# A two-layer attention and state-space trunk on one core: all hi and lo halves of q and k and all Toeplitz blocks moved to DMA transfers, a second token block sharing one PSUM bank, and a new instruction order

## The chip, the cores and the metric

The kernel runs on 1 core of a Trainium2 chip. The metric is the device time of one execution in microseconds (us), and lower is better. Before the change the median of three executions is 1128.52 us (1127.23 to 1130.73).

## The reference

The model is two post-norm layers on x of 512 tokens by 1024 features, float32. Cut to what matters:

```python
for l in range(2):
    h = x @ w_in[l]                                   # 1024 -> 2048
    q, k, v, u = jnp.split(h, [512, 1024, 1536], axis=-1)
    # attention: 4 heads, each with two maps of width 64; rotary on q and k; causal
    a = softmax(q0 @ k0.T / 8) - lam * softmax(q1 @ k1.T / 8)
    attn_out = rms_norm(a @ v, subln_g[l]) * (1 - lam_init)
    # S5: 32 groups of 16 channels, a complex diagonal state of 64 each, then GELU and GLU
    states = associative_scan(a_bar, einsum(u, b_bar))
    y = gelu(real(einsum(states, c)) + d_skip * u)
    ssm_out = y * sigmoid(y @ glu_w[l] + glu_b[l])
    mix = concat([attn_out, ssm_out]) @ w_out[l]
    x = layer_norm(ALPHA * x + mix, ln1_g[l], ln1_b[l])
    ff = square(relu(x @ w_ff1[l])) @ w_ff2[l]        # 1024 -> 4096 -> 1024
    x = layer_norm(ALPHA * x + ff, ln2_g[l], ln2_b[l])
```

## The kernel before

**Arithmetic.** Large products run as three fp32r matmuls, a.hi b.hi + a.hi b.lo + a.lo b.hi (`mm3`). A weight tile of 128x1024 is loaded into a `raw` buffer, rounded by ScalarE to `whi`, and its remainder becomes `wlo` in one of three ways, chosen by a letter: V (VectorE subtracts), P (GpSimd subtracts), A (ScalarE writes -hi and a GpSimd-issued accumulating DMA adds raw). The letters of the projections stand in `PLAN["lo"]`, of w_ff1 in `flo` (by i mod 4), of w_ff2 in `glo` (by the product m of a Strassen-like scheme of seven products) and `elo`, of w_out in `nlo`.

**Stages of a layer.** The projection list `back` names units: q and k of head h (`qkproj`, lines 1022 to 1068), v (`vproj`), u (`uproj`), and the GLU (`glu`). Between them come the attention units (`attn_u`, line 1110: head h, token block b of 128 queries), and the S5 units (`ssm_pars`, `ssm_outp`, `ssm_a`, `ssm_b`, `ssm_c`). Then come w_out with the first LayerNorm, and the feed-forward part in 8 chunks, each of four `ffone` (w_ff1) and seven `fftwo` (w_ff2) units, the last one `ffend` with the second LayerNorm.

**q and k.** After the projection ScalarE copies the PSUM bank to `src`, four DMAs swap 32-row blocks into `swp`, and VectorE makes the rotary result in three operations. The split into hi and lo halves for the two maps has two forms, chosen by `PLAN["qm"][l]`, first letter q and second k. In form A ScalarE casts 64-row pieces into the `xq` tiles (two for q, four for k), VectorE makes two 64-row remainders, and for k GpSimd clears two halves. In form D ScalarE casts all 128 rows once, VectorE makes one 128-row remainder, and DMAs from the SP queue put the 64-row pieces into their places: four for q, eight for k. Before, layer 0 has D for q and A for k, and layer 1 has A for both.

**Toeplitz blocks.** `ssm_outp` (line 976) fills `mx` with shifted copies of a 128-row block m3. In form A of `PLAN["mm"]` these are six ScalarE copies of 32 rows per call; in form D three DMAs.

**Banks of the attention.** Each map's scores get a PSUM bank of 512 columns. For blocks b below `PLAN["one"]` both maps share one bank: then one mask matmul and one VectorE maximum serve both.

**Order.** All instructions are recorded as `Op` objects with predecessors (`Rec.add`), then a list scheduler (`Rec.run`) simulates five queues with the durations of `Rec.cost` (DMA: lines 291 to 300, contention between the two DMA queues: lines 482 to 488) and issues in the order of the simulated starts. Each queue is in order on the chip. Priorities are shifted by hand-set tables: `pri` by unit, `fine` by instruction, `ao`, `so`, `ap`, `sp`, `po` by kind of unit, and the places of the units in the list by `att` and `s5`. `PE.matmul` fillers on the tile `wz` are added where the simulation leaves TensorE idle (`fill`).

Of the kernel before, what the change touches and what calls it, by code (L numbers as in the profile page):

```python
# [46 lines left out]
    "att": [[8, 11, 15, 19], [8, 12, 15, 18]],  # L47
    "s5": [[1, 13], [10, 14]],
    "bufs": {"slot": 13, "mh": 2, "y": 3, "xq": 13, "at": 4, "rt": 5, "u": 4},
    "ps": {"acc": 2, "sc": 4, "s5": 2},  # L50
    "lo": ["AAAVAAPAAAAVAAAAAAAA", "AAAAAAAAAAAAAPAVAAVP"],
    "eng": {"rope": ["VVV", "VVV"], "tab": ["VVVVVV", "VVVVVV"], "cg": ["VVVV", "VVVV"], "ch": ["VVVV", "VVVV"], "sa": ["PV", "VP"], "sb": ["VVVVVV", "VVVVVV"]},
    "flo": "VPVV",
    "nlo": "APVAVPVA",
    "glo": "APVVAAV",
    "seq": "f m1 m7 f m2 m4 f m6 f m5 m3",
    "elo": "VVVV",
    "wb": 4,
    "s5o": "p1 p0 o0 a0 b0 a1 c0 p2 o1 a2 b1 b2 c1 p3 o2 a3 b3 c2 o3 c3",
    "swq": "S",  # L60
    "ao": [-6000, -8000],
    "so": [2000, 17000],
    "ap": [56500, 92750],
    "sp": [27000, 25000],
# [9 lines left out]
    "po": 10000,  # L74
    "m3": 4,
    "pri": {"1a30": [150500, -9500], "1q1": [18500, 116500], "1v1": [-17500, 5000], "0ssm_a0": [2500, 74000], "0ssm_a1": [43000, -11000], "0ssm_a2": [57000, 85500], "0ssm_a3": [22500, 64500], "0ssm_b0": [2500, -20000], "0ssm_b1": [-4000, 37500], "0ssm_b2": [-500, 43500], "0ssm_b3": [14000, -60500], "0ssm_c0": [40000, 62000], "0ssm_c1": [53500, -21500], "0ssm_c2": [1500, 53500], "0ssm_c3": [58000, 90000], "0ssm_outp0": [-10500, 69500], "0ssm_outp1": [11000, 46500], "0ssm_outp2": [12000, -8000], "0ssm_outp3": [0, 55500], "0ssm_pars0": [-8000, 64000], "0ssm_pars1": [-6000, 13500], "0ssm_pars2": [10500, 43500], "0ssm_pars3": [1000, 30000], "1a10": [64000, 53500], "0a10": [89500, -22000], "0a22": [54500, 10000], "0q1": [-5000, 7500], "0q2": [19500, -19500], "0q3": [-14000, -14000], "0g1": [-28000, 41000], "1ssm_outp3": [-16000, -86000], "0u2": [37500, 17000], "0u3": [98500, 23500], "1a02": [144000, -41500], "1a31": [110000, 103000], "1a21": [80000, 8500], "1a03": [188000, 64500], "1a11": [94500, 72500], "1a13": [76000, -18500], "1a20": [135500, -91500], "1a22": [73500, 7500], "1a23": [185000, -24500], "1a32": [71500, 28000], "1a33": [105000, 129500], "1q3": [-39500, 10000], "0k0": [22500, -9500], "0k2": [-11500, -22000], "0k3": [5500, 25500], "1ssm_load2": [-29500, 49000], "1ssm_a0": [-11000, 39000], "0g3": [-69000, 40500], "0u0": [19000, -33500], "0u1": [64000, -10500], "1u0": [30000, -43500], "1u2": [11000, -7500], "1e3": [17000, 15500], "1a01": [147000, 78000], "0q0": [-1500, 5000], "0v0": [-5500, 55500], "0v1": [87500, 5000], "1e0": [-88000, -24500], "0v2": [55000, 47500], "0a12": [57500, 7000], "0a01": [91000, -21500], "0e1": [14500, 13500], "1ssm_b3": [30500, -18500], "1e1": [17500, 42500], "1g3": [-78500, 97000], "1g1": [22000, 119000], "1ssm_b2": [-75500, 68000], "0a13": [29000, 3500], "1a00": [103000, 29500], "1a12": [81500, 10500], "1v3": [72500, -37500], "1e2": [-44500, -13500], "1k2": [44500, 125500], "1ssm_outp1": [7000, -60500], "1ssm_a1": [22500, 0], "1ssm_a2": [3500, -24500], "1ssm_a3": [-13500, -24000], "1ssm_b0": [46000, 56500], "1ssm_b1": [-76000, -78000], "1ssm_c0": [0, -8500], "1ssm_c1": [26000, 19000], "1ssm_c2": [-21500, 21500], "1ssm_c3": [3500, -9000], "1ssm_load1": [8000, 13000], "1ssm_load3": [-2500, -13500], "1ssm_outp2": [-39500, 42500], "0k1": [-11000, -7500], "0v3": [118000, 30000], "0a31": [-38500, -27000], "0a03": [-10500, 4500], "0a30": [-4000, 47000], "1g0": [-56500, -27000], "1q0": [18000, -49500], "1q2": [87000, 38000], "0a02": [-2500, 30500], "1v2": [13500, -39000], "0e0": [-11000, 28500], "0e3": [27500, 50500], "0g0": [-81500, 59500], "1k0": [-1500, 9000], "1k1": [-11500, -27500], "0g2": [18000, 20000], "0a11": [10500, 36000], "1v0": [17000, 27000], "0e2": [-11500, 75500], "0a33": [76500, 11000], "1g2": [-32000, 19000], "1u3": [-29500, -5500], "0a32": [56000, 49000], "0a00": [44000, -48500], "1k3": [-3500, 35500], "0a20": [91500, 70000], "0a21": [9000, 66500], "0a23": [18000, 53500], "1u1": [-500, -9000]},
# [7 lines left out]
    "qm": ["DA", "AA"],  # L84
    "mm": ["A", "A"],
    "cc": ["AA", "AA", "AA", "AA"],
    "one": 1,
# [100 lines left out]
class Rec:  # L188
# [97 lines left out]
    def cost(self, op, views):  # L286
# [1435 lines left out]
```

## Time and profile before

| | us |
|---|---|
| median of 3 executions | 1128.52 |
| profiled execution, its own time | 1130.64 |
| its span, first to last instruction | 1128.9 |
| TensorE busy in the span | 1101.6 |
| VectorE busy | 919.5 |
| ScalarE busy | 609.3 |
| GpSimd busy | 199.0 |

The page gives busy time of each engine; the stretches are read from the table of windows, what an engine waited for from the lines of the timeline that carry a bracket, and the chain of waits goes back from the end of a stretch to what released each step. PE is TensorE, DVE VectorE, ACT ScalarE, POOL GpSimd, SP the queue that issues most DMAs. Nearly all instructions carry one line number (L534, where a record is replayed), so tiles are told apart by name: `ps_acc`, `ps_sc` and `ps_s` are PSUM banks, `xq` the halves of q and k, `rt` the rotary buffers, `mx` the Toeplitz blocks, `nm` the maxima.

### The profile page before, as it was taken

To read this page: it belongs to the slowest core of one execution; us is meant where nothing else is said; L and a number is where in the kernel's file an instruction comes from. 1 tells how busy PE (TensorE), PEld (TensorE's weight loads), DVE (VectorE), ACT (ScalarE), POOL (GpSimd) and SP (SyncE) were. 2 spreads that over 40 slices of the span, in tenths; PEclk is the share of its full clock that TensorE was granted. 3 is DMA by queue.
4 is the path that set the end of the run, shared out by engine and by line. 5 is a ranking of instruction groups with operands and counts; after the bars stand their busy time and mean duration, and the time that the engine had idled before them with its cause. 6 is when DMAs were issued, how large, how long until landed. Compare 5 with 4: busy or idle time off the path is not lost.

```text
span 1128.9 us, 15944 instructions
## 1 busy us (share of the span) xinstructions
PE 1101.6 (98%) x5738; PEld 929.7 (82%) x5738; DVE 919.5 (81%) x1575; ACT 609.3 (54%) x1060; POOL 199.0 (18%) x180
## 2 busy tenths in 40 slices
PE   9999989999999999999998999999999999999996
PEld 6889867898888888888788878888988888888885
DVE  7999998888778877877973789857778779778877
ACT  6557878246454464455343767952455445454440
POOL 1112111121211211211021221113112103103101
PEclk9999989999999999999999999999999999999999
DMA  9755645334555455465788764652444554565341
GB/s 312 193 138 109 161 124 155 116 112 115 147 159 131 122 164 134 119 178 148 224 226 208 179 163 106 194 145 81 141 131 131 149 149 119 144 159 148 105 130 74
DMA packets 59582, 167.73 MB, mean 149 GB/s; under 512 B 7408, under 2 KB 11888, under 8 KB 59504
## 3 DMA queue, kind: packets, MB, share of 16 engines
q1 hardware_dynamic: 48848, 127.92, 35.6%
q0 software_dynamic: 10656, 38.80, 18.6%
q8 instruction: 45, 0.74, 0.3%
q14 instruction: 33, 0.27, 0.1%
HBM read 112.17 MB, written 9.44 MB: 108 GB/s over the span
## 4 chain that ended last, share of the span: by engine, by line
PE 85%; DVE 6%; DMA 6%; ACT 3%; issue 1%; SPq 0%; POOL 0%; DVEq 0%; POOLq 0%; ACTq 0%
PE ps_acc L534 45%; PE ps_sc L534 28%; PE ps_s L534 12%; DVE slot L534 2%; DMA wlo<-raw 2%; DVE xq L534 1%; DMA rt<-rt 1%; DVE rt L534 1%; DMA raw<-in_w_v_dram 1%; DMA raw<-in_w_u_dram 1%; DMA keep<-xq 1%; DMA xq<-rt 1%; ACT at L534 0%; DMA slot<-in_xt_dram 0%; ACT whi L534 0%
## 5 line engine op out<-in xcount | busy, mean ns | idle before, releaser
L534 ACT CAST whi<-raw 128x1024 fp32r<-128x1024 f32 x222 | 233.3, 1051 | 284.2 <-PE ps_acc L534 177.9
L534 PE MATMUL ps_acc<-xTh,wlo 128*128 128x512 f32 (+1 forms) x712 | 268.5, 378 | 3.0 <-DMA wlo<-raw 1.9
L534 PE MATMUL ps_acc<-xTh,whi 128*128 128x512 f32 (+1 forms) x712 | 269.9, 380 | 0.7 <-ACT xTh L534 0.6
L534 PE MATMUL ps_acc<-xTl,whi 128*128 128x512 f32 (+1 forms) x712 | 268.7, 379 | 0.5 <-DVE xTl L534 0.5
L534 PE MATMUL ps_sc<-whi,slot 128*128 128x512 f32 x784 | 251.4, 390 | 1.3 <-DVE xq L534 1.3
L534 DVE TENSOR_TENSOR wlo<-raw,whi 128x1024 fp32r<-128x1024 f32 x114 | 139.0, 1226 | 56.6 <-ACT whi L534 56.6
L534 PEld LDWEIGHTS ps_sc<-whi,slot 128*128 128x128 f32 x784 | 147.1, 188 | 32.6 <-DVE xq L534 1.3
L534 POOL DMA_DIRECT2D wlo<-raw x74 | 65.0, 879 | 523.1 <-ACT rt L534 168.6
L534 PEld LDWEIGHTS ps_acc<-xTh,wlo 128*128 128x128 f32 x712 | 134.1, 188 | 26.7 <-DMA wlo<-raw 3.4
L534 PEld LDWEIGHTS ps_acc<-xTh,whi 128*128 128x128 f32 x712 | 134.0, 188 | 25.4 <-ACT xTh L534 1.8
L534 PEld LDWEIGHTS ps_acc<-xTl,whi 128*128 128x128 f32 x712 | 134.2, 188 | 24.2 <-DVE xTl L534 1.9
L534 PE MATMUL ps_sc<-wlo,slot 128*128 128x512 f32 x392 | 152.7, 390 | 0.0
L534 DVE TENSOR_TENSOR slot<-slot 128x512 fp32r<-128x512 f32 (+4 forms) x143 | 105.9, 755 | 7.8 <-ACT slot L534 7.0
L534 POOL TENSOR_TENSOR wlo<-raw,whi 128x1024 fp32r<-128x1024 f32 x34 | 85.0, 2501 | 151.5 <-ACT whi L534 124.2
L534 DVE TENSOR_TENSOR xq<-xq,ps_sc 128x512 f32<-128x512 f32 x124 | 83.6, 681 | 25.8 <-PE ps_sc L534 25.8
L534 ACT ACTIVATE wlo<-raw 128x1024 fp32r<-128x1024 f32 x74 | 78.3, 1060 | 29.0 <-PE ps_acc L534 18.5
L534 PEld LDWEIGHTS ps_sc<-wlo,slot 128*128 128x128 f32 x392 | 73.6, 188 | 15.2
L534 DVE TENSOR_TENSOR raw<-raw 128x1024 f32<-128x1024 f32 x56 | 68.2, 1218 | 14.2 <-DMA raw<-in_w_ff_dram 13.5
L534 ACT CAST slot<-slot 128x512 fp32r<-128x512 f32 x56 | 34.6, 618 | 50.9 <-DVE slot L534 48.4
L534 PE MATMUL ps_acc<-wlo,xTh 128*128 128x256 f32 (+1 forms) x176 | 55.6, 322 | 3.1 <-DMA wlo<-raw 3.1
L534 PE MATMUL ps_acc<-whi,xTh 128*128 128x256 f32 (+1 forms) x176 | 56.3, 324 | 0.2 <-ACT rt L534 0.2
L534 PE MATMUL ps_acc<-whi,xTl 128*128 128x256 f32 (+1 forms) x176 | 55.9, 321 | 0.0
(228 smaller groups left out, 1846.1 us busy)
## 6 DMA issues: line engine op xcount, KB each, us to landing
raw<-in_w_ff_dram SPq DMA_DIRECT2D x128, 512.0 KB, 3.6
wlo<-raw POOLq DMA_DIRECT2D x74, 512.0 KB, 5.3
raw<-in_w_qk_dram SPq DMA_DIRECT2D x16, 512.0 KB, 5.0
raw<-in_w_out_dram SPq DMA_DIRECT2D x16, 512.0 KB, 3.6
raw<-in_w_u_dram SPq DMA_DIRECT2D x8, 512.0 KB, 4.8
raw<-in_w_v_dram SPq DMA_DIRECT2D x8, 512.0 KB, 7.0
rt<-rt SPq DMA_DIRECT2D x64, 64.0 KB, 2.8
at<-in_ln_dram SPq DMA_DIRECT2D x16, 256.0 KB, 3.9
```

What stands on the lines that cost most here:

```text
L534: getattr(self.real[op.eng], op.name)(*[_real(x) for x in op.a], **{n: _real(x) for n, x in op.k.items()})
```

## The change

Both letters of `qm` become D in both layers, `mm` becomes D in both layers, and `one` goes from 1 to 2, so block b = 1 also shares a bank. The scheduler's DMA prices are replaced: less per row, more latency (1463 for 1000 ns), other fixed parts, and a contention rule that delays both queues instead of one. The tables `pri` and `fine` are new throughout, and `att`, `s5`, `ao`, `so`, `ap`, `sp` and `po` have new values: the S5 units of layer 1 start at place 4 of the list instead of 10, those of layer 0 at 4 instead of 1. Of the letters for `wlo`, those used change so: `flo` first V to A and second P to V, `glo` m = 4 V to P and m = 6 A to P, last used `nlo` A to P, `elo` first V to A. (The changed letters of `lo` stand at units that do not read them: v with an odd number and g3.) `hv` and `vw` are new switches at values that keep the code as it was.

```diff
-    "att": [[8, 11, 15, 19], [8, 12, 15, 18]],
-    "s5": [[1, 13], [10, 14]],
+    "att": [[8, 12, 15, 19], [8, 12, 15, 18]],
+    "s5": [[4, 14], [4, 13]],
...
-    "flo": "VPVV",
-    "nlo": "APVAVPVA",
-    "glo": "APVVAAV",
+    "flo": "AVVV",
+    "nlo": "APVAVPVP",
+    "glo": "APVPAPV",
...
-    "elo": "VVVV",
+    "elo": "AVVV",
...
-    "s5o": "p1 p0 o0 a0 b0 a1 c0 p2 o1 a2 b1 b2 c1 p3 o2 a3 b3 c2 o3 c3",
+    "s5o": "p1 p0 o0 a0 b0 a1 c0 p2 o1 b1 a2 b2 c1 p3 o2 a3 b3 c2 o3 c3",
...
-    "ao": [-6000, -8000],
-    "so": [2000, 17000],
-    "ap": [56500, 92750],
-    "sp": [27000, 25000],
+    "ao": [-6000, 20000],
+    "so": [2000, 21000],
+    "ap": [52500, 80750],
+    "sp": [31000, 29000],
...
-    "po": 10000,
+    "po": -6000,
...
-    "qm": ["DA", "AA"],
-    "mm": ["A", "A"],
+    "qm": ["DD", "DD"],
+    "mm": ["D", "D"],
...
-    "one": 1,
+    "one": 2,
...
-            op.move = rows * runs / 16 * (47.0 + o.idx.size * 4 / runs / 35.0) * (2.0 if e != "DMA" else 1.0)
-            op.fix = 50.0 if e != "DMA" or not on[0] else 990.0 if on[1] else 890.0
-            return (660.0 if rows < 128 else 500.0) if e == "DMA" else 1030.0, 1000.0 + op.fix + 1.3 * op.move
+            op.move = rows * runs / 16 * (33.0 + o.idx.size * 4 / runs / 32.1) * (1.7 if e != "DMA" else 1.0)
+            op.fix = 30.0 if e != "DMA" or not on[0] else 750.0 if on[1] else 586.0
+            return (660.0 if rows < 128 else 500.0) if e == "DMA" else 1030.0, 1463.0 + op.fix + 1.3 * op.move
...
-                q, z = ("POOL", "DMA") if e == "POOL" else ("DMA", "POOL")
-                b = max(move[q], op.t1 + 1000.0)
-                move[q] = b + op.move + min(op.move, max(0.0, move[z] - b))
+                q, z, r, u = ("POOL", "DMA", 0.515, 0.734) if e == "POOL" else ("DMA", "POOL", 0.266, 0.485)
+                b = max(move[q], op.t1 + 1463.0)
+                both = max(0.0, min(op.move / r, move[z] - b))
+                move[q] = b + op.move + both * (1 - r)
+                move[z] += both * u
```

## Rows read from the trace of the kernel before

**Rows 1.** The page, busy time, share of the span and instructions of each engine.

```profile
PE 1101.6 (98%) x5738; PEld 929.7 (82%) x5738; DVE 919.5 (81%) x1575; ACT 609.3 (54%) x1060; POOL 199.0 (18%) x180
```

**Rows 2.** Windows by stage: length, busy us (instructions) by engine, clock, DMA share, GB/s.

```profile
0.00:40.00 40.00, 36.89 (x181) 27.82 (x182) 32.01 (x140) 23.66 (x36) 6.53 (x12) 1.00 0.90 282
40.00:140.00 100.00, 99.73 (x653) 87.83 (x652) 98.09 (x239) 69.89 (x163) 16.13 (x22) 1.00 0.58 143
140.00:180.00 40.00, 34.48 (x195) 27.33 (x193) 34.70 (x84) 33.19 (x95) 6.07 (x9) 0.87 0.54 147
...
240.00:527.00 287.00, 287.00 (x1343) 240.72 (x1342) 228.82 (x289) 146.50 (x194) 50.11 (x34) 1.00 0.51 138
527.00:600.00 73.00, 70.75 (x423) 62.18 (x422) 53.88 (x101) 30.75 (x51) 8.88 (x11) 1.00 0.77 224
600.00:680.00 80.00, 72.98 (x461) 64.44 (x460) 59.63 (x117) 52.40 (x105) 15.74 (x23) 0.98 0.72 181
680.00:760.00 80.00, 79.73 (x486) 67.31 (x485) 63.17 (x132) 64.27 (x167) 13.39 (x15) 1.00 0.55 146
```

**Rows 3.** Timeline of PE, 140 to 160 us: start, us, what [idle before, releaser].

```profile
150.85 1.05 PE L534 MATMUL ps_sc<-cs,at 128*128 128x128 f32 x3 [2.48 <-ACT at L534]
158.35 0.80 PE L534 MATMUL ps_acc<-y,whi 128*128 128x512 f32 x1 [1.20 <-DVE y L534]
```

**Rows 4.** Chain of waits, 140 to 160 us: start, us, what.

```profile
148.61 0.61 ACT xq L534
...
151.70 0.30 ACT mx L534
...
154.27 0.30 ACT mx L534
...
156.07 0.62 ACT xq L534
```

**Rows 5.** Timeline of PE, 600 to 670 us.

```profile
614.47 0.39 PE L534 MATMUL ps_acc<-wlo,xTh 128*128 128x256 f32 x1 [3.10 <-DMA wlo<-raw]
...
667.16 0.50 PE L534 MATMUL ps_acc<-xTh,wlo 128*128 128x512 f32 x1 [1.93 <-DMA wlo<-raw]
```

**Rows 6.** Chain of waits, 527 to 760 us: the long transfers.

```profile
603.60 10.82 DMA wlo<-raw
...
658.59 8.52 DMA wlo<-raw
```

**Rows 7.** Tiles rt and mx: duration ns min/median/max, first and last start, forms.

```profile
L534 ACT CAST xq<-rt x40: 607/617/632, 35.1 to 719.3; 64x512 fp32r<-64x512 f32 x40
...
L534 DVE TENSOR_TENSOR xq<-rt,xq x24: 675/687/1574, 36.0 to 719.2; 64x512 fp32r<-64x512 f32 x24
L534 DVE TENSOR_TENSOR rt<-rt x20: 681/691/694, 28.1 to 715.0; 128x512 f32<-128x512 f32 x16, 128x512 fp32r<-128x512 f32 x4
L534 SPq DMA_DIRECT2D xq<-rt x16: 461/526/1527, 31.2 to 166.5; - x16
...
L534 ACT CAST rt<-rt x4: 610/621/631, 28.9 to 162.8; 128x512 fp32r<-128x512 f32 x4
...
L534 ACT COPY mx<-m x56: 290/296/302, 64.6 to 691.7; 32x128 f32<-32x128 f32 x48, 128x128 f32<-128x128 f32 x8
```

**Rows 8.** DMA issues of the page: out<-in, queue, xcount, KB each, median us to landing.

```profile
wlo<-raw POOLq DMA_DIRECT2D x74, 512.0 KB, 5.3
...
xq<-rt SPq DMA_DIRECT2D x16, 128.0 KB, 5.7
```

**Rows 9.** Groups by form, whole span: busy us, mean ns | idle before.

```profile
L534 DVE TENSOR_REDUCE nm<-ps_sc 128x1 f32<-128x512 f32 x16 | 10.9, 682 | 0.1
...
L534 DVE TENSOR_REDUCE nm<-ps_sc 128x1 f32<-128x256 f32 x16 | 6.6, 420 | 3.1 <-PE ps_sc L534 2.9
```

**Rows 10.** Windows of 40 us in the second feed-forward part.

```profile
840.00:880.00 40.00, 40.00 (x178) 33.14 (x177) 32.77 (x38) 19.35 (x25) 10.20 (x6) 1.00 0.55 152
880.00:920.00 40.00, 40.00 (x178) 33.09 (x177) 31.70 (x40) 20.24 (x25) 5.04 (x4) 1.00 0.52 130
```

More of the change, by code (lines that the diff above doesn't have):

```diff
@@ L46 @@
     ],
[L47 to L48 removed]
+    "att": [[8, 12, 15, 19], [8, 12, 15, 18]],
+    "s5": [[4, 14], [4, 13]],
     "bufs": {"slot": 13, "mh": 2, "y": 3, "xq": 13, "at": 4, "rt": 5, "u": 4},
     "ps": {"acc": 2, "sc": 4, "s5": 2},
[L51 removed]
+    "lo": ["AAAVAAVAAAAVAAAAAAAA", "AAAAAAAAAAAAAAAVAAVA"],
     "eng": {"rope": ["VVV", "VVV"], "tab": ["VVVVVV", "VVVVVV"], "cg": ["VVVV", "VVVV"], "ch": ["VVVV", "VVVV"], "sa": ["PV", "VP"], "sb": ["VVVVVV", "VVVVVV"]},
[L53 to L55 removed]
+    "flo": "AVVV",
+    "nlo": "APVAVPVP",
+    "glo": "APVPAPV",
     "seq": "f m1 m7 f m2 m4 f m6 f m5 m3",
[L57 removed]
+    "elo": "AVVV",
     "wb": 4,
[L59 removed]
+    "s5o": "p1 p0 o0 a0 b0 a1 c0 p2 o1 b1 a2 b2 c1 p3 o2 a3 b3 c2 o3 c3",
     "swq": "S",
[L61 to L64 removed]
+    "ao": [-6000, 20000],
+    "so": [2000, 21000],
+    "ap": [52500, 80750],
+    "sp": [31000, 29000],
     "pw": -6000,
@@ L1072, in vproj @@
     def vproj(l, z):
-        if z % 2 == 0:
-            v_w[l] = [w for c in range(2) for w in wsplit(w_v[l, z // 2, c], 1024, 4, lo_mode(l, f"v{z}") if l or z else "V")]
-        acc = bank(bt(l, f"v{z}"))
-        for b in range(2):
-            xb_ = xblk(2 * (z % 2) + b)
-            for k in range(KD):
-                mm3(acc[:, 256 * b:256 * b + 256], xb_[k], v_w[l][k], k == 0, k == KD - 1)
+        if PLAN["vw"][l]:
+            if z == 0:
+                v_w[l] = [w for c in range(4) for w in wsplit(w_v[l, c], 1024, 2, lo_mode(l, f"v{c}"))]
+            acc = bank(bt(l, f"v{z}"))
+            for k, x_ in enumerate(xblk(z)):
+                mm3(acc, x_, v_w[l][k], k == 0, k == KD - 1)
+        else:
+            if z % 2 == 0:
+                v_w[l] = [w for c in range(2) for w in wsplit(w_v[l, z + c], 1024, 4, lo_mode(l, f"v{z}") if l or z else "V")]
+            acc = bank(bt(l, f"v{z}"))
+            for b in range(2):
+                xb_ = xblk(2 * (z % 2) + b)
+                for k in range(KD):
+                    mm3(acc[:, 256 * b:256 * b + 256], xb_[k], v_w[l][k], k == 0, k == KD - 1)
         if z % 2 == 0:
@@ L1117, in vj @@
         def vj(j):
+            if PLAN["vw"][l]:
+                return v_t[l, j][:, h * P:(h + 1) * P]
             i = 256 * (j % 2) + 128 * (h % 2)
@@ L1399, in trunk @@
         else:
-            us = [z for z in PLAN["back"][l] if z[0] in "uqk"][:4]
-            for z, acc in zip(us, xprod([(z, t_) for z, t_ in zip(us, BANKS4)], l, HALVES)):
+            us = [z for z in PLAN["back"][l] if z[0] in "uqk"][:PLAN["hv"]]
+            for z, acc in zip(us, xprod([(z, t_) for z, t_ in zip(us, BANKS4)], l, HALVES) if us else []):
                 pre[l, z] = acc
@@ L1667, in _layout @@
     o["w_qk"] = w[:, :, :, 0:2].transpose(0, 4, 3, 2, 1, 5).reshape(L, 4, 2, 128, 1024)
-    o["w_v"] = (a["w_in"][:, :, 1024:1536].reshape(L, 2, 4, 128, 2, 256).transpose(0, 4, 1, 3, 2, 5)
-                .reshape(L, 2, 2, 128, 1024))
+    wv = a["w_in"][:, :, 1024:1536]
+    o["w_v"] = np.stack([wv[l].reshape(4, 2, 128, 512).transpose(0, 2, 1, 3).reshape(4, 128, 1024) if PLAN["vw"][l] else
+                         wv[l].reshape(2, 4, 128, 2, 256).transpose(3, 0, 2, 1, 4).reshape(4, 128, 1024) for l in range(L)])
     o["w_u"] = a["w_in"][:, :, 1536:].reshape(L, 8, 128, 4, 128).transpose(0, 3, 2, 1, 4).reshape(L, 4, 128, 1024)
```

6 lines of the change are left out of this document (4 added, 2 removed).

## The prediction, made before the changed kernel was run

> **What bounds the kernel now.** I read the busy line of the page first, then the table of windows, then the idle marks on TensorE's timeline, and last the chain of waits in the stretches where TensorE loses time. TensorE is busy 1101.6 us [rows 1], so the most that a new order can give back is what it loses, and the windows tell where [rows 2]. In the feed-forward part it is busy 287.00 of 287.00 us: no edit there can shorten the kernel, it can only spoil it. The losses stand in four places: 3.11 us in 0 to 40, with the DMA engines 0.90 busy (the first weights); 40 - 34.48 = 5.52 us in 140 to 180, and there the mean granted clock is 0.87, that is about 0.26 x 40 = 10.4 us at 1.2 instead of 2.4 GHz, worth up to 0.13 x 40 = 5.2 us more; 73 - 70.75 = 2.25 us in 527 to 600; 80 - 72.98 = 7.02 us in 600 to 680, where clock 0.98 is worth 1.6 us. The start is set by transfers that stay. Without it 5.52 + 5.2 + 2.25 + 7.02 + 1.6 = 21.6 us can be won, and this is the cap of every gain below. What the last LayerNorm does after the last matmul isn't touched.
>
> The two large places have different causes. In 40 to 140 DVE is busy 98.09 of 100 us while TensorE is at 99.73 [rows 2]: VectorE's queue is full and falls behind, and the hole opens behind that stretch. In the hole's chain ScalarE stands too: the four casts into xq, between 148.61 and 156.07, and seven copies into mx, between 151.70 and 154.27 [rows 4], and the largest idle mark, 2.48 us, was ended by ACT [rows 3]. The clock fell behind that mark. In 600 to 680 it is transfers: two marks of 3.10 and 1.93 us were ended by the accumulating transfer of a wlo [rows 5], which took 10.82 and 8.52 us from issue to landing [rows 6] against a median of 5.3 [rows 8].
>
> **The change part by part.**
>
> k and q by transfers. A k unit in form A costs ScalarE 4 x 0.617 us and VectorE 2 x 0.687; in form D one cast of 128 rows, 0.621, and one remainder of 128 rows, 0.691 [rows 7]. So each k saves ScalarE 1.85 and VectorE 0.68 us; a q, with two casts, saves 0.61 and 0.68. Layer 0 changes four k: ScalarE 7.4, VectorE 2.7 us. Layer 1 changes four k and four q: ScalarE 9.8, VectorE 5.5 us. GpSimd loses its 16 memsets of k. What is added goes to the SP queue: eight issues of 0.526 us per k and four per q [rows 7], so 4.2 and 2.1 us of issue, and the landing, 5.7 us in the median [rows 8]. From the finished rotary result, a k is then there after 0.62 + 0.69 + 4.2 + 5.7 = 11.2 us in place of about 2.5 us of casts and the last remainder, 3.2 us: 8.0 us later. A q goes from 1.2 + 0.7 = 1.9 us to 0.62 + 0.69 + 2.1 + 5.7 = 9.1 us: 7.2 us later. These issues stand in SP's in-order queue: while the first of them waits for the cast, the weight loads behind it wait too, and TensorE waits for those once the five raw buffers are used up. Added are 4 x 8 issues in layer 0 and 4 x 12 in layer 1, 80 x 128 KB. I take the latency as hidden in most units, since the q of layer 0 go this way already and TensorE is busy 99.73 of 100 us in the stretch that holds most of them [rows 2]. Bounds: nothing, and the 2.5 us mean of the two marks of [rows 5] for each of the 12 units, 30 us.
>
> Toeplitz blocks by transfers. Six copies of 0.296 us go from ScalarE [rows 7] in eight calls: 7.1 us in each layer. Three small DMAs per call come to SP, 24 in all; the block is read by the last S5 matmuls, well behind. Taken as nothing on SP's side, with at most 24 x 0.526 = 12.6 us of issue time there.
>
> Two blocks in one bank. One mask matmul of 5738 less in each of eight heads, and a maximum over 512 columns at 0.682 us in place of two over 256 at 0.420 [rows 9]: 0.16 us each, 1.3 us of VectorE in all. Against it the first exponential of such a block waits 0.26 us longer. I take both together as 0.
>
> Letters of wlo. By loop counts VectorE does 16 remainders fewer, GpSimd 14 more, ScalarE with the accumulating transfer 2 more. Nearly all of these are in the feed-forward part. There a 40 us window with 10.20 us of GpSimd and one with 5.04 have the same TensorE, 40.00 of 40.00 [rows 10]; the new letters make every chunk like the fuller one. So 0, with DVE's idle 7 to 8 us in each such window as the cover; without it, the 5.2 us difference per second chunk would be the price.
>
> The Trainium skill, "SBUF — State Buffer", section "SBUF: two separate sides", speaks against this part: GpSimd and a VectorE operation with two SBUF inputs lock the shared port pair out for each other for a whole instruction. By it the 14 added subtractions would also block VectorE. What the rows of the fuller window show is that TensorE doesn't feel it, so the sum stays.
>
> Order. This is the part without an instruction to price. In layer 0 I take from the hole what leaves its two engines: of the chain's ACT pieces 4 x 0.617 + 7 x 0.296 = 4.5 us, less the one cast of 0.6 that stays, and the VectorE backlog, shorter by 2.7 + 4 x 0.16 = 3.3 us. That is 7.2 us of a hole worth 5.52 + 5.2 = 10.7. Something else will be late next (the DVE chain itself, or the new transfers of the last head), so I count 5.5, near the amount of idle time. Bounds 0 and 10.7. In layer 1 the two long transfers of [rows 6] outlast the median by 5.5 and 3.2 us. An order made with contention on both queues places their consumers later or their issue earlier. I take the marks, 3.10 + 1.93, and half of the 1.6 us of clock: 5.8, and give 2.0 back for the 48 new transfers in a stretch where the DMA engines are already 0.72 busy: 3.8. Bounds 8.6 + 2.25 = 10.9 us won, and the 30 us above lost.
>
> Sum: 5.5 + 3.8 = 9.3 us. The profiled execution took 1130.64 us (span 1128.9); it becomes 1121.3. The median of the three runs lies 2.1 us lower, so I forecast 1119 us.
>
> **The rivals.**
>
> Late transfers (slower). The new halves land after the order expects them, TensorE's in-order queue stops at the first score matmul of a head, and everything behind it stops too. Each unit costs the 2.5 us of [rows 5]; four units (10 us) eat the gain, and that is the point from which it decides. With six of the twelve, +15 - 9.3 = +6: 1134 us. For it: 8.0 us more latency per k, the marks of [rows 5] that are transfers already, DMA share 0.72 in layer 1 and 0.90 in the first 40 us. Against it: the new order knows these transfers, and layer 0's q lose little.
>
> The hole moves (no change). DVE stays the bound of layer 0, since only 3.3 us of its 98 go, and what layer 1 gains at two marks it loses at other transfers: between 1126 and 1130, 1128 us.
>
> The holes close (large gain). The cap of 21.6 us less a tenth: 19.5 us, 1109. For it: in 600 to 680 DVE and ACT are busy only 59.63 and 52.40 of 80 us [rows 2], room for S5 work that starts earlier in the list.
>
> The change doesn't do what it says: the transfers might cost as much queue as they free. The 80 transfers take no engine's busy time, so this comes back to the first rival.
>
> **How the numbers follow.** Forecast (1113 to 1125): 0.49. Large gain (below 1113): 0.14. No change (1125 to 1132): 0.18. Late transfers (above 1132): 0.19. A difference of 0.3% (3.4 us) is about what a measurement of this kernel tells from no change, so faster is below 1125.1, slower above 1131.9: 0.63, 0.18 and 0.19. The range takes in most of both outer cases: 1108 to 1134.
>
> **What would show it.** Right: in 140 to 180 the clock is back near 1.00 and TensorE's idle time there under 2 us; ACT xq and ACT mx pieces are gone from the chain; in 600 to 680 no idle mark over 2 us ended by a wlo transfer; the feed-forward windows unchanged at 40.00 of 40.00. Wrong: idle marks on score matmuls ended by the transfers xq<-rt (late transfers); marks ended by DVE at the same place with the same size (the hole moves); TensorE below 40.00 in feed-forward windows, ended by POOL (the letters).

## The result and the profile after

The changed kernel takes 1135.73 us in the median (1133.61 to 1136.44) against 1128.52: the ratio is 1.0057, with a 95% interval of 1.0039 to 1.0076. It is slower by about 6.4 us, where 9.3 us less were forecast. The profiled execution took 1135.95 us, its span is 1134.2 us against 1128.9. In what follows a ratio is always to the kernel before, and "+6.4 us" is the ratio's excess times 1128.5.

The page after, busy time by engine and the packets of the DMA engines:

```profile
PE 1103.5 (97%) x5748; PEld 931.7 (82%) x5748; DVE 893.3 (79%) x1539; ACT 578.7 (51%) x986; POOL 228.0 (20%) x180
...
DMA packets 68191, 180.07 MB, mean 159 GB/s; under 512 B 9104, under 2 KB 15120, under 8 KB 68112
```

VectorE has 26 and ScalarE 31 us less to do than in [rows 1], as the change says, and yet the kernel is longer. The windows of [rows 2] again, in the same columns (stage limits shift by up to some 10 us against the kernel before):

```profile
0.00:40.00 40.00, 36.94 (x175) 28.32 (x175) 32.62 (x143) 23.33 (x35) 5.91 (x11) 1.00 0.88 278
40.00:140.00 100.00, 96.83 (x619) 85.17 (x620) 93.90 (x225) 58.02 (x132) 12.45 (x18) 0.98 0.69 171
140.00:180.00 40.00, 34.86 (x227) 28.35 (x227) 34.10 (x83) 27.48 (x86) 6.06 (x6) 0.91 0.66 175
240.00:527.00 287.00, 286.74 (x1357) 241.05 (x1356) 218.17 (x280) 141.82 (x185) 69.73 (x41) 1.00 0.52 139
527.00:600.00 73.00, 69.77 (x393) 59.84 (x392) 56.87 (x106) 33.74 (x53) 9.91 (x12) 1.00 0.76 215
600.00:680.00 80.00, 75.24 (x496) 67.86 (x496) 53.42 (x108) 42.77 (x84) 15.90 (x21) 0.98 0.93 222
680.00:760.00 80.00, 78.04 (x469) 64.97 (x469) 61.91 (x127) 55.40 (x148) 9.09 (x9) 1.00 0.74 189
```

TensorE's first number, beside [rows 2], tells where. The hole of layer 0 is as large as it was by this number (34.86 for 34.48 us). The stretch ahead of it, 40 to 140, which had lost almost nothing, now loses 3.17 us of idle time and 0.02 of the clock. In layer 1, 600 to 680 gains 2.3 us, and its two neighbours lose 1.0 and 1.7.

The number of the hole flatters the change, because it counts the fillers, the matmuls on `wz` that compute nothing. The hole's window for this tile alone (TensorE, its weight loads, VectorE), before and after:

```profile
140.00:180.00 40.00, 1.81 (x12) 1.09 (x12) 0.00 (x0) 0.87 0.54 147
140.00:180.00 40.00, 6.41 (x37) 4.27 (x38) 0.00 (x0) 0.91 0.66 175
```

Without fillers TensorE is busy 32.67 us there before and 28.45 after. The new order doesn't close the hole; it puts more fillers into it.

Which stage the loss comes from can be counted from the starts of TensorE's matmuls, without fillers and mask matmuls, 5608 in both kernels. The 1100th, at about the end of layer 0's attention, starts at 216.80 us before and 220.95 after, 4.15 later; the 2500th, near the end of the feed-forward part, 4.35 later; the 3900th, at 756.51 us before, 5.77; the last, 5.25. So about four fifths of the 5.3 us by which the span grew are lost ahead of layer 0's feed-forward part, and layer 1 adds about one.

Who TensorE waited for, in total, number of times and longest (us):

```profile
PE ps_sc L538 <- DMA xq<-rt: 3.9, 5, 1.5
PE ps_acc L538 <- ACT rt L538: 3.3, 1, 3.3
PE ps_s L538 <- DMA mx<-m: 3.1, 2, 2.6
...
PE ps_acc L538 <- DMA wlo<-raw: 1.4, 1, 1.4
```

The wlo transfers of [rows 5] are nearly gone, 1.4 us in place of 5.0. In their place stand the transfers that the change adds, 3.9 us on scores (1.3 before, from the q of layer 0) and 3.1 on Toeplitz blocks. The longest single mark, 3.3 us, is ended by ScalarE; it comes back among the experiments. The two places where the added transfers bite in layer 0, on TensorE's timeline:

```profile
49.57 0.87 PE L538 MATMUL ps_sc<-xq 128*128 128x128 f32 x5 [1.46 <-DMA xq<-rt]
...
155.42 0.46 PE L538 MATMUL ps_s<-mx,u 128*128 128x128 f32 x2 [2.61 <-DMA mx<-m]
```

And the chain of waits that ends in them (start, us, what; SPq is SP issuing a transfer):

```profile
41.43 1.69 SPq L538
43.16 1.94 SPq L538
45.21 4.32 DMA xq<-rt
49.57 3.21 PE ps_sc L538 x16
...
149.95 0.62 SPq L538
150.62 4.67 DMA mx<-m
155.42 0.46 PE ps_s L538 x2
```

The first score matmul starts at 49.57 us, where the kernel before had it at 38.35. Most of these 11 us are no loss: TensorE works on projections meanwhile and is idle 1.46 us before it. In the hole, where ScalarE's pieces stood in [rows 4], the chain now goes through SP and a Toeplitz transfer of 4.67 us. So the pieces that the prediction wanted out of the chain are out, and the hole stayed.

### The profile page after: what moved, and what is told of

The parts are those of the page before. It is cut to its first block, busy times and chain, and to the rows that moved or that the text cites. A ratio compares the mean times of both kernels' runs of the same rounds, so it can differ in the third digit from the quotient of the medians.

```text
span 1134.2 us, 16051 instructions
## 1 busy us (share of the span) xinstructions
PE 1103.5 (97%) x5748; PEld 931.7 (82%) x5748; DVE 893.3 (79%) x1539; ACT 578.7 (51%) x986; POOL 228.0 (20%) x180
## 4 chain that ended last, share of the span: by engine, by line
PE 80%; DMA 7%; DVE 6%; ACT 3%; SPq 2%; issue 1%; POOL 0%; DVEq 0%; ACTq 0%; POOLq 0%
PE ps_acc L538 42%; PE ps_sc L538 26%; PE ps_s L538 12%; SPq L538 2%; DMA xq<-rt 2%; DVE slot L538 2%; DMA wlo<-raw 1%; DVE rt L538 1%; DMA raw<-in_w_v_dram 1%; DMA mx<-m 1%; DMA raw<-in_w_qk_dram 1%; DVE at L538 1%; ACT whi L538 1%; DMA slot<-in_xt_dram 1%; DVE nm L538 0%
## 5 line engine op out<-in xcount | busy, mean ns | idle before, releaser
L538 POOL TENSOR_TENSOR wlo<-raw,whi 128x1024 fp32r<-128x1024 f32 x48 | 120.5, 2511 | 225.3 <-ACT whi L538 167.8
L538 DVE TENSOR_TENSOR wlo<-raw,whi 128x1024 fp32r<-128x1024 f32 x98 | 119.2, 1218 | 56.4 <-ACT whi L538 55.2
L538 DVE TENSOR_TENSOR slot<-slot 128x512 fp32r<-128x512 f32 (+4 forms) x143 | 124.9, 887 | 15.2 <-ACT slot L538 14.8
```

Of the source, the lines that this page charges most:

```text
L538: getattr(self.real[op.eng], op.name)(*[_real(x) for x in op.a], **{n: _real(x) for n, x in op.k.items()})
```

## The experiments

**Theories.** A: the added transfers themselves are the loss, because they land later than the engines would have had the data, and SP's in-order queue makes them wait for one another. B: the loss is VectorE or ScalarE as before, and the new order only moved it. C: the transfers are harmless, and the loss is in the new order.

The new order is one fixed list, so a change can be put into the kernel before without it, and taken out of the changed kernel without touching it. Each run below keeps the list of one of the two kernels and replaces instructions when they are issued. The edits are shown shortened.

### One part at a time in the old order

Toeplitz blocks only: 24 transfers in place of 48 ScalarE copies.

```diff
+            if op.name == "copy" and op.a[0].t.key[1][:2] == "mx" and rows(op.a[0]) == 32:
+                if op.a[0].p[0] == 0:
+                    self.real["DMA"].dma_start(out=mx[0:(t + 1) * 32, t], in_=m3[(3 - t) * 32:128])
+                continue
```

> The kernel before in its own order, but the 48 ScalarE copies into mx are replaced by the changed kernel's 24 transfers from the SP queue, issued where the first copy stood. The prediction took these as costing nothing: then the time is that of the run with the copies on GpSimd, 1126 to 1129 us. If the transfers land late, as the 2.61 us mark on the first S5 matmul of the changed kernel suggests, 1129 to 1133 us, with idle marks on ps_s ended by the transfers mx<-m.

1125.88 us, ratio 0.9977 (0.9964 to 0.9991): 2.6 us faster than the kernel before, and faster than the changed one. In this order the transfers cost less than ScalarE's copies did, though not nothing: one mark of 1.0 us on `ps_s` is ended by `mx<-m`.

Halves only: the eight (k) or four (q of layer 1) transfers with one cast and one remainder.

```diff
+            if op in units.get(op.group, ()):         # form A: casts, remainders, memsets
+                if op is units[op.group][0]:
+                    A.copy(swp.bitcast(F32R), src); V.tensor_tensor(src.bitcast(F32R), src, swp, op=SU)
+                    for t_, o, w, p in moves:          # 8 for k, 4 for q
+                        self.real["DMA"].dma_start(out=t_[o], in_=w[p])
+                continue
```

> The kernel before in its own order, but the halves of k in both layers and of q in layer 1 are made as in the changed kernel: one cast, one remainder, then eight or four transfers from the SP queue, all issued where the first cast stood (80 transfers). The order was made without them, so this is the price of the bare latency. By the late-transfers rival: 2.5 us for each of 12 units, 1128.5 + 30 = about 1158 us, with marks on ps_sc ended by the transfers xq<-rt. If the latency is hidden even so and the freed 17 us of ScalarE and 8 us of VectorE count: 1122 to 1129 us.

1155.30 us, ratio 1.0235 (1.0198 to 1.0271): +26.5 us. TensorE's waits in it begin with:

```profile
PE ps_sc L578 <- DMA xq<-rt: 16.7, 7, 4.2
```

The landing of these transfers, from the page's DMA issues (out<-in, queue, count, KB, median us):

```profile
xq<-rt SPq DMA_DIRECT2D x96, 128.0 KB, 2.4
```

Seven marks of 2.4 us in the mean: the size that the late-transfers rival took from [rows 5]. The landing is only 2.4 us, not the 5.7 of [rows 8], and the price comes all the same: the issues are the larger part of the latency. Eight took 4.95 us on SP's timeline from 36.79 us.

The marks of 16.7 us are not the whole price. TensorE's idle time grows by 14.5 us, from 27.3 to 41.8, and its busy time by 9.4, from 1101.6 to 1111.0, with the same 5738 matmuls: the mean granted clock fell from 0.992 to 0.982, most of all behind the marks in layer 1 (0.98 before):

```profile
600.00:680.00 80.00, 69.58 (x449) 62.63 (x448) 44.30 (x92) 39.23 (x83) 14.48 (x18) 0.91 0.81 197
```

Nor is the price of 26.5 us that of the latency alone. The edit puts the cast, the remainder and all issues at the place of the first cast, so VectorE's queue now waits for casts too, five times and 4.7 us in all (L570 is the cast, L573 the remainder):

```profile
DVE rt L573 <- ACT rt L570: 4.7, 5, 2.2
```

The four k of layer 0 alone (the same edit for groups that begin with 0):

> The kernel before in its own order, with the halves by transfers for the four k of layer 0 alone (32 transfers). If each unit costs the same, 26.3 us over 12 units gives 2.2 us each: four units are 8.8 us, about 1138 us. If VectorE and ScalarE were what held the hole of layer 0, the time they save there (2.7 and 7.4 us) counts against it: 1129 to 1133 us.

1134.31 us, ratio 1.0056 (1.0037 to 1.0074): +6.3 us, 1.6 us a unit. By the difference, the eight units of layer 1 carry the other 20 us, 2.5 us each. The time that ScalarE and VectorE save in layer 0 doesn't pay for four units.

Both parts:

> The kernel before in its own order with both kinds of transfers of the two runs before: all operations of the change except the shared bank of block 1 and the letters of wlo, without the new order. If the two parts add: the sum of their two differences from the kernel before. The changed kernel at 1135.7 us less this time is then what the new order gives back (or takes).

1161.31 us, ratio 1.0292 (1.0264 to 1.0321): +33.0 us, where 26.5 - 2.6 = 23.9 were the sum. The two first lines of TensorE's waits show what was added:

```profile
PE ps_sc L586 <- DMA xq<-rt: 15.8, 8, 3.9
PE ps_s L586 <- DMA mx<-m: 5.8, 1, 5.8
```

The Toeplitz blocks, nearly harmless alone, make TensorE wait 5.83 us beside the halves. To see whether the queue does it, only these 24 went to ScalarE's queue:

```diff
-                    self.real["DMA"].dma_start(out=mx[0:(t + 1) * 32, t], in_=m3[(3 - t) * 32:128])
+                    self.real["ACT"].dma_start(out=mx[0:(t + 1) * 32, t], in_=m3[(3 - t) * 32:128])
```

> The kernel before in its own order with both kinds of transfers, but the 24 into mx are issued from ScalarE's queue, the 80 of the halves from SP's as before. With both on SP the time was 1161.3 us, and the two differences taken apart add to 1128.8 + 26.5 - 2.6 = 1152.7 us. If the Toeplitz transfers were late because they stood behind the halves in SP's queue: the mark of 5.83 us ended by mx<-m goes and the time is 1152 to 1156 us. If it was the landing or the data that was late: 1159 to 1163 us with the mark as it was.

1155.72 us, ratio 1.0232 (1.0207 to 1.0257): +26.2 us, 6.8 less than with all on SP. SP's and ScalarE's issues in the hole, and the first S5 matmul, on the timeline:

```profile
155.69 3.80 SPq L586 DMA_DIRECT2D rt<-rt  x4
...
160.62 5.14 SPq L575 DMA_DIRECT2D xq<-rt  x8
...
162.30 0.56 ACTq L584 DMA_DIRECT2D mx<-m  x1
...
166.85 0.77 PE L586 MATMUL ps_s<-mx,u 128*128 128x128 f32 x2 [0.44 <-DMA mx<-m]
```

On SP these would have stood behind the eight issues of a k that hold the queue from 160.62 to 165.76. On the other queue they go out in the middle of them, and the mark falls from 5.83 to 0.44 us. This is shown, then, for the old order: halves and Toeplitz blocks collide in SP's queue, and theory A holds for this part.

Half of the halves' issues on ScalarE's queue:

```diff
-                    for t_, o, w, p in moves:
-                        self.real["DMA"].dma_start(out=t_[o], in_=w[p])
+                    for n, (t_, o, w, p) in enumerate(moves):
+                        self.real["ACT" if n % 2 else "DMA"].dma_start(out=t_[o], in_=w[p])
```

> The kernel before in its own order with all 80 transfers of the halves, but every second one issued from ScalarE's queue, so that the last of a k is issued after four issues instead of eight. If the price is the serial issue on SP (8 x 0.53 us per k), about half of the 26 us goes: 1142 us. If it is the landing (2.4 us) and the one wait of SP's queue for the remainder, little goes: 1150 to 1156 us. If the waits that now stand in ScalarE's queue cost more than they save: above 1156 us.

1156.61 us, ratio 1.0249 (1.0223 to 1.0275): no better than one queue. Its waits tell why:

```profile
PE ps_sc L578 <- ACT at L578: 9.5, 6, 4.8
PE ps_sc L578 <- DMA xq<-rt: 6.0, 4, 2.9
```

The waits for the halves fall from 16.7 to 6.0 us, so the serial issue does make most of them. But the issues now hold ScalarE's queue and the softmax behind them: the waits for `ACT at` rise from 3.6 to 9.5 us. At the longest of these, 4.8 us, VectorE's factor `f` is done at 161.45 us, and ScalarE scales `at` by it only at 163.32, behind its four issues:

```profile
159.83 2.91 ACTq L575 DMA_DIRECT2D xq<-rt  x4
...
161.30 0.15 DVE L578 TENSOR_TENSOR f<-f,ri 128x4 f32<-128x4 f32 x1
...
163.32 1.26 ACT L578 ACTIVATE at<-at,f 128x128 f32<-128x128 f32 x4
```

The time is given back, not won.

### Back to engines in the new order

Halves, Toeplitz blocks, or both copied by GpSimd at the place of the transfer:

```diff
+            if op.name == "dma_start" and op.eng == "DMA" and to == "xq":     # or to[:2] == "mx", or both
+                for r in range(0, n, h):                                     # h = 64, for mx 32
+                    self.real["POOL"].tensor_copy(o[r:r + h], i[r:r + h])
+                continue
```

> The changed kernel in its own order, but the 80 new transfers of halves of q and k (all k, and q of layer 1) are GpSimd copies of 64x512 at the same place of the order. Late transfers: TensorE's waits for xq<-rt (3.9 us in 5 marks) and the late first score (49.6 us against 38.3) go, so 4 to 8 us less than the changed kernel's 1135.7, 1128 to 1132. Order alone (the new order is worse whatever fills the halves): no change, 1134 to 1137. GpSimd takes on about 80 x 0.55 = 44 us; if that delays its own subtractions, slower than 1137.

> The changed kernel in its own order, but the 24 transfers of Toeplitz blocks are 48 GpSimd copies of 32x128 at the same place. Late transfers: the marks ended by mx<-m (2.6 and 0.5 us) go, so 2 to 4 us less than 1135.7, 1132 to 1134. Order alone: 1135 to 1137.

> Both edits together: 104 transfers fewer, in the changed kernel's own order. Late transfers: the sum of the two, 1125 to 1130, at or below the kernel before (1128.5). Order alone: 1134 to 1137.

1146.15 us, ratio 1.0137 (1.0118 to 1.0156), for the halves; 1133.32, 1.0025 (1.0012 to 1.0039), for the Toeplitz blocks; 1148.74, 1.0164 (1.0148 to 1.0180), for both. Against GpSimd copies the Toeplitz transfers cost the changed kernel 0.0032 x 1128.5 = 3.6 us, between intervals that just touch: with them its 2.61 us mark goes. The halves say less: a GpSimd cast of 64x512 took 0.80 us in the median and up to 2.15, and TensorE's wait for `ACT rt` grew from 3.3 to 6.4 us, so this form is worse for reasons of its own. What the halves by transfer cost the changed kernel is therefore not isolated.

Form A of the kernel before, ScalarE casts and VectorE remainders, at the places of the new order, and the same with ScalarE's Toeplitz copies:

```diff
-                    Q.dma_start(out=f[i][o].bitcast(F32), in_=w[p])
+                    A.copy(t_[p], src[p]); A.copy(t_[o], src[p])
+                    V.tensor_tensor(u_[p], src[p], t_[p].bitcast(F32), op=SU); G.memset(u_[o], 0.0)
```

> The changed kernel in its own order, but the halves of all k and of layer 1's q are made as before (form A: 64-row casts by ScalarE, 64-row remainders by VectorE, GpSimd clears) at the places of the cast and the remainder, without the 80 transfers. Transfers as the cause: the late first score and the waits for xq<-rt go, 1126 to 1131, though ScalarE gets 17 us and VectorE 8 us back. Order alone as the cause: 1134 to 1138.

> The same, and the Toeplitz blocks are ScalarE copies of 32 rows again at the places of their transfers: the new order, bank and letters without any of the 104 new transfers. Transfers as the cause: 1124 to 1129, at or below the kernel before. Order alone: 1134 to 1138.

1137.75 us, ratio 1.0079 (1.0055 to 1.0103), and 1144.95, 1.0132 (1.0117 to 1.0147). Giving ScalarE its old work back in the new order doesn't help, and with the Toeplitz copies it is clearly slower: the largest wait of both is now `ACT rt`, 9.0 us in three marks. The new order uses the freed ScalarE. With the 80 transfers of halves gone, the mark of `mx<-m` in the hole stays all the same in the first:

```profile
156.90 0.77 PE L575 MATMUL ps_s<-mx,u 128*128 128x128 f32 x2 [3.03 <-DMA mx<-m]
```

So neither list tells what the other's operations would cost in a list of their own; the four corners are:

| | operations of before | with both kinds of transfers |
|---|---|---|
| old order | 0 | +33.0 us |
| new order | +14.9 us | +6.4 us |

(Both corners of the new order also have the shared bank of block 1 and the new wlo letters, and in the old order's right corner the cast, the remainder and the transfers stand at the first cast's place.) Beside the transfers, the new order with its places, bank and letters takes back 33.0 - 6.4 = 26.6 us. Theory C falls as it was put: the transfers aren't harmless, and beside them the order is not the loss but what nearly pays for it. It has waits of its own, though. In each of the nine runs with the new order TensorE waits 3.3 to 9.0 us for `ACT rt` and 1.4 to 4.5 for a remainder (`DVE wlo`); in the kernel before these are 0.4 and nothing, in the other runs of the old order up to 5.2 and 0.2.

### What an issue on SP costs

The casts by GpSimd as above, and the 80 transfers still issued and moved, into a place that nobody reads:

```diff
+                    self.real["POOL"].tensor_copy(o, i)
+                    op.k["out"] = self.spill.pop()
```

> As with the halves by GpSimd copies, but the 80 transfers are issued as well, at the same place and from the same source, into DRAM that nobody reads: the traffic, the SP queue's issues and the held buffers stay, only the wait of the score matmuls for a landing goes. Late landing: as the run with copies alone, 1128 to 1132. Crowded queue (the transfers hold up weight loads, swaps and remainders): back at the changed kernel's time, 1134 to 1137. Order alone: 1134 to 1137, and the run with copies alone too.

1144.39 us, ratio 1.0127 (1.0110 to 1.0144): no slower than the 1.0137 without them. Issues and bytes that nobody waits for cost nothing that shows here. Every transfer of a half as two of 32 rows, 80 issues more:

```diff
+                for r in (0, 32):
+                    self.real["DMA"].dma_start(out=o[r:r + 32], in_=i[r:r + 32])
```

> The changed kernel in its own order, each of the 80 new transfers of halves as two of 32 rows: the same bytes and packets, 80 more issues on SP at 0.59 us, 47 us. Serial issue on SP as the cause: 5 to 12 us more than the changed kernel, 1141 to 1148. Landing or bytes as the cause, or order alone: 1134 to 1138.

1173.82 us, ratio 1.0391 (1.0367 to 1.0415): 0.0334 x 1128.5 = 38 us more than the changed kernel, for 47 us more of issue time on SP (266.8 to 313.6). Where TensorE does wait for the issues, most of their time passes into the kernel:

```profile
PE ps_sc L544 <- DMA xq<-rt: 17.6, 10, 6.1
PE ps_s L544 <- DMA mx<-m: 5.5, 3, 3.2
```

These marks are 16 us more than in the changed kernel. As with the halves in the old order, the clock adds to them: 0.978 for 0.992, and TensorE's busy time is 1117.3 us for 1103.5.

Every second of the 80 from ScalarE's queue:

```diff
+                turn += 1
+                self.real["ACT" if turn % 2 else "DMA"].dma_start(out=o, in_=i)
```

> The changed kernel in its own order, every second of the 80 new transfers of halves issued from ScalarE's queue in place of SP's. Serial issue on SP as the cause: a k is complete about 2.4 us earlier and what is queued behind it too, 2 to 6 us less than the changed kernel, 1130 to 1134. Landing or bytes, or order alone: 1134 to 1138. ScalarE held up by its own issues: slower than 1138.

1141.02 us, ratio 1.0095 (1.0071 to 1.0119): no faster than the changed kernel, by the ratios 4.3 us slower, with intervals that overlap. As in the old order, xq<-rt waits shrink (3.9 to 2.2 us) and ScalarE's grow (ACT rt 3.3 to 5.2). SP's load alone is not the price; it is the load ahead of somebody who waits.

### The two holes that the forecast counted on

**Layer 0.** The Toeplitz copies by GpSimd in the old order, without a transfer:

```diff
+            if op.eng == "ACT" and op.name == "copy" and op.a[0].t.key[1][:2] == "mx" and rows(op.a[0]) == 32:
+                self.real["POOL"].tensor_copy(op.a[0], op.a[1]); continue
```

> The kernel before in its own order, but the 48 ScalarE copies of 32 rows into mx are made by GpSimd at the same place of the order: no transfer is added. It tests the prediction's step for the hole of layer 0, that ScalarE pieces which leave the hole's chain (7 mx copies of 0.296 us, 2.1 us) shorten it. By that step: 1128.5 - 2.1, about 1126.5 us, and the idle mark of 2.48 us ended by ACT is gone. If VectorE alone holds the hole, or something else is next in line: 1128 to 1130 us, with marks of the same sum ended by DVE or by GpSimd.

1129.48 us, ratio 1.0001 (0.9987 to 1.0014): ScalarE is rid of the same copies as in the run with transfers, and nothing is won. Beside the Toeplitz transfers, four ScalarE casts of the last heads' k, or all eight VectorE remainders of layer 0's k, to GpSimd:

```diff
+            if op.eng == "ACT" and op.a[0].t.key[1] == "xq" and op.group in ("0k2", "0k3") and op.a[0].p[0] != op.a[1].p[0]:
+                self.real["POOL"].tensor_copy(op.a[0], op.a[1]); continue
...
+            if op.eng == "DVE" and op.a[0].t.key[1] == "xq" and op.group in ("0k0", "0k1", "0k2", "0k3"):
+                self.real["POOL"].tensor_tensor(*op.a, **op.k); continue
```

> The kernel before in its own order, Toeplitz blocks by 24 transfers, and in addition the four cross-half casts of k of heads 2 and 3 in layer 0 (0.617 us each on ScalarE) made by GpSimd at the same place. If ScalarE's casts hold the hole of 140 to 180 us, as the prediction's chain had it: 1 to 2.5 us less than with the Toeplitz transfers alone, 1123.5 to 1125 us. If VectorE holds it: no difference, 1125 to 1127 us, or more where GpSimd is slower than ScalarE was.

> The kernel before in its own order, Toeplitz blocks by 24 transfers, and in addition the eight 64-row remainders of k in layer 0 made by GpSimd instead of VectorE (8 x 0.687 = 5.5 us less on VectorE by 160 us). If VectorE's full queue is what opens the hole, TensorE gets back a part of these 5.5 us: 1121 to 1124 us, with more than 35 us of TensorE in 140 to 180 us. If VectorE does not hold it: 1125 to 1127 us. If GpSimd's slower remainder makes the score matmuls late: marks on ps_sc ended by POOL xq, 1127 us or more.

1128.57 us, ratio 0.9990 (0.9976 to 1.0004), and 1128.02, 0.9991 (0.9978 to 1.0004): neither is faster than the Toeplitz transfers alone (0.9977). The window of the hole with the casts on GpSimd, then with the remainders there:

```profile
140.00:180.00 40.00, 34.26 (x194) 26.67 (x193) 36.25 (x85) 30.70 (x87) 7.31 (x11) 0.87 0.57 155
```

```profile
140.00:180.00 40.00, 33.91 (x200) 27.35 (x199) 34.97 (x82) 32.14 (x90) 11.66 (x13) 0.87 0.56 151
```

TensorE is busy 33.91 to 34.62 of these 40 us in the five kernels of the old order compared (before 34.48, Toeplitz on GpSimd 34.22, by transfers 34.62, and these two), 1.81 us of it fillers in each. Taking pieces from ScalarE's or VectorE's queue didn't move it. In all five the same mark stays, a `ps_sc` matmul that waits 2.5 to 3.4 us for `ACT at`, a link of the softmax. In the run with only the Toeplitz transfers these lines lead to it:

```profile
147.53 1.04 POOL L542 TENSOR_TENSOR f<-f,mhalf 128x4 f32<-128x4 f32 x1 [3.50 <-DVE f L542]
148.60 0.63 ACT L542 ACTIVATE slot<-slot 128x512 f32<-128x512 f32 x1
148.74 0.16 DVE L542 TENSOR_TENSOR f<-f,ri 128x4 f32<-128x4 f32 x1
149.13 1.26 ACT L542 ACTIVATE at<-at,f 128x128 f32<-128x128 f32 x4
149.57 0.91 PE L542 MATMUL ps_sc<-cs,at 128*128 128x128 f32 x3 [2.48 <-ACT at L542]
```

The factor `f` passes through GpSimd and is done on VectorE at 148.89 us. ScalarE scales `at` by it at 149.13, without idle time, because its own queue holds S5 work (`slot`) until then. So the two queues reach this point within 0.3 us of each other, and taking work from one of them can win no more than that at this link. All seven `mx` copies of [rows 4] start after the mark of 150.85 us in [rows 3] has ended; they can't have made it.

The two GpSimd runs also add a delay of their own at this very place. Here are the same `f` and the scaling, with the casts and then with the remainders on GpSimd:

```profile
149.13 0.66 POOL L543 CAST xq<-rt 64x512 fp32r<-64x512 f32 x1
149.24 0.57 DVE L545 TENSOR_TENSOR f<-f,ri 128x4 f32<-128x4 f32 x1
149.84 1.28 ACT L545 ACTIVATE at<-at,f 128x128 f32<-128x128 f32 x4 [0.72 <-DVE f L545]
```

```profile
150.65 3.15 POOL L543 TENSOR_TENSOR xq<-rt,xq 64x512 fp32r<-64x512 f32 x2
150.84 1.23 DVE L545 TENSOR_TENSOR f<-f,ri 128x4 f32<-128x4 f32 x1
152.10 1.28 ACT L545 ACTIVATE at<-at,f 128x128 f32<-128x128 f32 x4 [0.76 <-DVE f L545]
```

ScalarE is free early and waits 0.7 us for `f`, which takes 0.57 and 1.23 us in place of 0.16: it ends 0.02 us behind the cast, and as closely behind the first of the two remainders. So these runs don't tell what a shorter queue alone would win. Whether the hole yields when both queues are relieved together, or the length of the softmax itself holds it, wasn't tried and stays open.

**Layer 1.** The Toeplitz transfers, and five remainders of the projections in layer 1 by VectorE in place of ScalarE and the accumulating transfer:

```diff
+            if op in drop:              # scale=-1.0 and its accumulating transfer, planned 590 to 620 us
+                V.tensor_tensor(lo, raw, hi.bitcast(F32), op=SU); continue
```

> The kernel before in its own order, with the Toeplitz blocks by 24 transfers (1125.9 us in that run) and in addition five remainders wlo of layer 1's projections (planned 590 to 620 us) made by one VectorE subtraction each instead of a ScalarE negation and an accumulating transfer. The prediction's mechanism for layer 1 was that late wlo transfers make TensorE wait. If so, the mark of 3.51 us ended by wlo<-raw near 612 us goes, and the clock of 600 to 620 us, 0.91, returns to 1.00: 3 to 5 us, about 1121 to 1123 us. If VectorE becomes late in its place (five times some 1.3 us): 1126 us or more.

1126.01 us, ratio 0.9973 (0.9959 to 0.9987): no gain over 1125.88. The windows show that the mark went and where the time went on:

```profile
600.00:620.00 20.00, 20.00 (x148) 18.88 (x147) 15.53 (x25) 7.40 (x10) 1.29 (x1) 1.00 0.57 165
620.00:640.00 20.00, 18.07 (x121) 15.54 (x119) 15.72 (x31) 11.18 (x30) 1.92 (x4) 1.00 0.42 132
640.00:680.00 40.00, 38.80 (x237) 33.61 (x238) 36.64 (x72) 27.02 (x51) 9.02 (x15) 1.00 0.67 169
```

600 to 620 is full at 20.00 us, clock 1.00, where the run with only the Toeplitz transfers has 16.49 us at 0.91. But 620 to 640 falls from 20.00 to 18.07, and 640 to 680 from 39.18 to 38.80: from 600 to 680 only 76.88 - 75.67 = 1.2 us are won. The next in line were softmax and copies (`ACT rt`, 2.7 us in three marks). The first 40 us of this profiled execution happen to be 2.9 us worse (TensorE 34.49 for 37.41), which is no part of the edit; the median shows no gain either.

## Why the prediction was wrong, point by point

- **The latency of the halves, "I take the latency as hidden in most units".** This is the step that failed. It was charged with 0 in layer 0 and 2.0 us in layer 1, because the four q of layer 0 went this way already. In the order as it was, the price is 26.5 us over 12 units, 2.2 each: the rival's 2.5 us a unit and the bound of 30 us were nearly right, the value taken was not. Some 15 us of it are added marks ended by the transfers (16.7 less the 1.3 of before); the rest is for the most part the lower clock behind them, to which the prediction gave no term, and some of it can be VectorE's waits at the moved places. The row it leaned on, TensorE at 99.73 of 100 us, shows no slack for eight more microseconds: with the four k of layer 0 alone by transfers the time rises by 6.3 us. What the new order can hide was no number of the trace of before, and I put it at almost everything; order, places, bank and letters together took back 26.6 of 33.0 us.
- **The sum.** Between the forecast of 9.3 us less and the 6.4 us more stand 15.7 us. Of these 9.3 are gains of layers 0 and 1 that in sum did not come. The other 6.4 are what new waits cost beyond those that went: of the transfers 3.9 us on scores and 3.1 on Toeplitz blocks, of the new order 3.3 for `ACT rt` and 1.4 for `DVE wlo`.
- **Late transfers as rival.** Its mechanism is what happened: marks on ps_sc ended by xq<-rt, in five places. Its 1134 us is near the 1135.7, but partly by luck: it had six of twelve units late at 2.5 us and 9.3 us of gains, whereas the marks of xq<-rt are only 3.9 us and the gains did not come.
- **Toeplitz transfers "taken as nothing on SP's side", "well behind".** Nearly right alone (-2.6 us in all, one mark of 1.0) and wrong beside the halves in the old order: a call's transfers stand behind eight issues of a k in the same queue, 5.83 us of wait. The prediction had named SP's in-order queue for weight loads and then not asked it about mx. The 2.61 us mark of the changed kernel is another matter. There the three issues go out at 149.35 us, behind loads and 3.7 us after the block was ready, and ahead of the next halves; they land 4.7 to 5.5 us later, and without the transfers of halves the mark is 3.03. So "well behind" failed there by the landing and by loads. With GpSimd copies in their place the changed kernel is 3.6 us faster.
- **Layer 0's hole, 5.5 us.** Nothing came: 34.48 to 34.86 us of TensorE, with 4.6 us more of fillers in it, clock 0.87 to 0.91. The ACT pieces in [rows 4] stood in the chain, but only two casts of them before the end of the mark in [rows 3]; the seven mx copies, 2.1 of the 4.5 us counted, come behind it. The clause "something else will be late next" was true and was given 1.7 of 7.2 us; it took nearly all. "The hole moves" was the better rival here.
- **Layer 1, 3.8 us.** The wlo marks went, as forecast (5.0 to 1.4 us), and 600 to 680 won 2.3 us. The neighbours lost 1.0 and 1.7. The run with the remainders on VectorE shows that removing such marks is worth 1.2 us even without the new transfers: the term was mis-sized by taking the marks at face value. It also left out the new order's own wait in this stretch, 3.3 us for `ACT rt` at 623.88.
- **Letters, feed-forward part.** 286.74 of 287.00 us of TensorE with GpSimd up from 50.11 to 69.73: taken as 0, it is 0.3 us, one mark ended by VectorE (`DVE xq`). The Trainium skill's rule on the port that GpSimd and VectorE share ("SBUF — State Buffer", "SBUF: two separate sides") can have cost TensorE at most this there, as the prediction judged. In layer 0's hole the trace of the run with casts on GpSimd agrees with it: VectorE's `f`, with two inputs, took 0.57 us in place of 0.16 beside such a cast.
- **Shared bank.** Taken as 0. No run separates it from the new order; it stays open.

## What to carry to other kernels

An order that is fitted to measured times has no slack for a longer latency: price a transfer that replaces a copy as issue times plus landing for each unit that TensorE reads, add what the clock loses behind a wait, and take "hidden" only where the trace shows the data lying ready for that long. Transfers that cost little alone can be late behind others in the same in-order queue, so count what stands ahead of each on its queue. A mark taken away is worth what is left after the next one in line, and busy time of TensorE counts as work only without its fillers. Here the part worth keeping was the small one, the Toeplitz transfers in the old order: 0.9977 (0.9964 to 0.9991), faster than both kernels.

## What the runs showed of the hardware

- SP issues one at a time and not at a fixed rate. In the changed kernel the sum is 266.8 us for 493 issues (before 186.5 for 389); a half's issue takes 0.595 us in the median and up to 1.94. Issues over 0.9 us come mostly while a GpSimd-issued accumulating transfer has packets under way: 42 of 139 then, 10 of 354 otherwise (before: 28 of 86, and 5 of 303). That the one causes the other wasn't tried.
- The landing of the same 64x512 transfer depends on its company: median 2.4 us in the run with the halves in the old order, 4.5 in the changed kernel, whose DMA share in 600 to 680 is 0.93 (0.72 before).
- ScalarE can issue such a transfer in 0.48 us in the median, but the issues stand in its queue with its other work: four of them held it for 2.91 us from 159.83 us in the run with two queues in the old order.
- Behind such waits TensorE's granted clock was lower. With the halves by transfers in the old order its mean granted clock is 0.982 for 0.992, and the same 5738 matmuls are busy 9.4 us longer.
- VectorE's `f` (128x4, two inputs) takes 0.14 to 0.17 us in most places, and 0.57, 0.86 to 0.88 and 1.23 where a GpSimd cast or two-input operation runs as it starts; it then ends 0.02 us behind that operation, in each of the nine cases of seven runs.
